# w_out and the second half of w_down: some pairs of row tiles by seven block products in place of eight

## The chip, the core and the metric

The kernel runs on one core of one Trainium2 chip. Five engines work side by side, each through its own queue of instructions: TensorE (PE, matmuls; PEld is its loading of the stationary operand), VectorE (DVE), ScalarE (ACT), GpSimd (POOL) and SyncE (SP, which here issues loads). Times are microseconds of one execution on the device. The metric is that time; before the change its median is 1509.69 us over three runs.

## The reference, cut to what matters

One decoder layer, 256 tokens, model width 2048, float32. The mixer's two halves (state space and attention, 2048 features each) are concatenated and projected by `w_out`; the MLP goes up to 8192 and down again:

```
y_mix = concatenate([y_ssm, y_att], axis=-1)        # (256, 4096)
mix   = einsum('bse,ed->bsd', y_mix, w_out)         # (256, 2048)
h     = h + rmsnorm(mix, norm_mix_post)
hdn   = relu(einsum('bsd,df->bsf', rmsnorm(h, norm_mlp_pre), w_up))
ff    = einsum('bsf,fd->bsd', hdn * hdn, w_down)    # 8192 -> 2048
h     = h + rmsnorm(ff, norm_mlp_post)
```

## The kernel before

Every large product keeps float32 accuracy by splitting both operands into a rounded part (hi, type fp32r) and the rest (lo), and adding three products: hi·hi, hi·lo, lo·hi. `split` (L122) makes the parts: ScalarE writes hi (L125), VectorE subtracts to get lo (L126). Activations are split once and kept: `uh`/`ul` in the tile `u2` (normalised input of a projection), `sh`/`sl` and `ah`/`al` (16 row tiles of 128 features each; `part(k)` finds row tile k of 32).

Weights stream. `fetch` loads two row tiles by 512 columns (512 KB) into one of four `raw` buffers; `weights` (L145) splits them into one of five `hi` and five `lo` buffers. All of that is given a high priority, so the scheduler puts it as far ahead in each queue as buffers let it.

`gemm_tokens` (L170) is the product with tokens in rows: for a block of 512 columns it takes two PSUM banks (one for each tile of 128 tokens) and goes through the row tiles in pairs (KB = 2): per pair 2 token tiles x 2 row tiles x 3 parts = 24 matmuls of 128x512 from two column blocks' view, 12 per column block. `w_out` and each half of `w_down` have 32 row tiles (16 pairs) and four column blocks. Where `lag` is given, the second token tile runs some pairs behind the first, so that the first one's end can be worked on early.

PSUM has eight banks: six in `pacc` (`bank`), two in `psm` (`psmall`). While `w_out`'s first column block runs, attention's last four heads are still going on: each head is a generator in `waiting`, and `pump` runs one step of one head after each pair of row tiles. Then attention's memory is given back and the pool `hp` opens on it: `h` (the residual stream, 2 MB), `mw` (the collected result), `wpost` (the norm's weights, 1 MB broadcast), and `r`, two tiles of 128x512. Their loads are issued by ScalarE (L679, L680).

For each finished column block of `w_out`, `mixed` (L636) sums the squares from PSUM on ScalarE and multiplies by `wpost` on VectorE. After the last one `residual` (L643) scales, adds to `h`, transposes it on TensorE and splits it into `u2` for `w_up`. The second half of `w_down` adds its column blocks to what the first half left in `mw`; `finish` (L716) does the last block and writes the output.

## Time and profile before

| | us |
|---|---|
| median of three runs | 1509.69 (1509.39 to 1510.25) |
| the profiled execution, its own time | 1508.91 |
| its span, first instruction to last | 1507.1 |
| matmuls recorded | 7725 |

The span is what the profile covers; the execution's own time is 1.8 us longer. In the rows of the profile, the first number of a timeline row is its start in us from the span's start, the second its duration in us; x4 means four instructions merged, the duration then runs from the first's start to the last's end. In a row of groups, the numbers behind the bar are busy us in total and mean ns of one. In a row of windows, each engine has its busy us and, in brackets, how many instructions; then come the granted clock of TensorE (1.00 is full), the DMA engines' busy share and GB/s. Where a window was asked for TensorE alone, its column is the only one. In a row of loads the last number is the median time from issue to landing.

### The profile page before, as it was taken

The page shows a single profiled execution, that of the slowest core. Times are in us where ns is not written, and L with a number is a line of the kernel's source. Part 1 is how long each engine was busy: PE and PEld are TensorE (multiplying, and loading weights), DVE is VectorE, ACT ScalarE, POOL GpSimd, SP SyncE. Part 2 cuts the span into 40 slices and gives each one's busy share as a digit, 9 for nine tenths or more (in the row PEclk, how much of TensorE's full clock was granted, in tenths as well). Part 3 has the DMA queues.
Part 4 walks back from the last instruction along what each step waited for, and adds up shares of the span by engine and source line. Part 5 has one row for each costly group of instructions (what it writes and reads, how often), then busy time and mean ns, then how long its engine had stood idle before and what let it go on. Part 6 is the DMA issues. An engine that isn't in the chain of part 4 may idle for free.

```text
span 1507.1 us, 20168 instructions
## 1 busy us (share of the span) xinstructions
PE 1493.2 (99%) x7725; PEld 1275.4 (85%) x7725; DVE 917.5 (61%) x1314; ACT 763.1 (51%) x1063; POOL 56.1 (4%) x73
## 2 busy tenths in 40 slices
PE   9999999999999999999999999999999999999997
PEld 8888888888888888888878888888888888888886
DVE  6988797886555565544457656644444665655444
ACT  7564665554545454544456555543444555544432
POOL 0002200220000000000000000000000000000000
PEclk9999999999999999999999999999999999999999
DMA  7665566556555655475556666555556666655553
GB/s 274 193 205 177 184 183 190 181 155 181 173 177 169 179 169 179 168 266 194 185 167 216 185 189 194 182 195 195 192 189 197 191 185 192 189 189 194 191 174 126
DMA packets 147841, 283.13 MB, mean 188 GB/s; under 512 B 11312, under 2 KB 14240, under 8 KB 147232
## 3 DMA queue, kind: packets, MB, share of 16 engines
q1 hardware_dynamic: 143312, 272.37, 57.4%
q10 hardware_dynamic: 4432, 9.48, 1.8%
q8 instruction: 60, 0.98, 0.3%
q14 instruction: 37, 0.30, 0.1%
HBM read 279.68 MB, written 2.13 MB: 187 GB/s over the span
## 4 chain that ended last, share of the span: by engine, by line
PE 96%; DVE 2%; DMA 1%; ACT 1%; issue 1%; SPq 0%; POOL 0%; POOLq 0%; DVEq 0%; ACTq 0%
PE acc L201 29%; PE acc L187 16%; PE acc L188 16%; PE acc L189 16%; PE acc L204 15%; PE ps L521 1%; DMA raw<-in_w_in_dram 1%; DVE lo L126 1%; PE ps L564 0%; PE ps L586 0%; ACT hi L125 0%; DMA raw_dt<-in_w_in_dram 0%; PE ps L477 0%; PE ps L563 0%; PE ps L587 0%
## 5 line engine op out<-in xcount | busy, mean ns | idle before, releaser
L126 DVE TENSOR_TENSOR lo<-raw,hi 128x1024 fp32r<-128x1024 f32 (+1 forms) x514 | 631.3, 1229 | 527.9 <-ACT hi L125 526.6
L125 ACT ACTIVATE hi<-raw 128x1024 fp32r<-128x1024 f32 (+1 forms) x514 | 542.5, 1056 | 637.7 <-PE acc L189 336.0
L201 PE MATMUL acc<-u,hi 128*128 128x512 f32 x1984 | 539.3, 398 | 1.3 <-DVE u L128 1.2
L201 PEld LDWEIGHTS acc<-u,hi 128*128 128x128 f32 x1984 | 344.8, 189 | 51.4 <-DVE u L128 1.4
L204 PEld LDWEIGHTS acc<-u,lo 128*128 128x128 f32 x1984 | 296.2, 189 | 36.9
L204 PE MATMUL acc<-u,lo 128*128 128x256 f32 x1984 | 305.4, 281 | 0.0
L187 PE MATMUL acc<-hi,sh 128*128 128x512 f32 x384 | 150.5, 392 | 0.0
L187 PE MATMUL acc<-hi,ah 128*128 128x512 f32 x384 | 149.9, 390 | 0.0
L188 PE MATMUL acc<-lo,sh 128*128 128x512 f32 x384 | 149.5, 389 | 0.0
L189 PE MATMUL acc<-hi,sl 128*128 128x512 f32 x384 | 149.4, 389 | 0.0
L189 PE MATMUL acc<-hi,al 128*128 128x512 f32 x384 | 149.4, 389 | 0.0
L188 PE MATMUL acc<-lo,ah 128*128 128x512 f32 x384 | 149.4, 389 | 0.0
L187 PE MATMUL acc<-hi,u 128*128 128x512 f32 x288 | 112.9, 393 | 0.3 <-ACT u L127 0.3
L189 PE MATMUL acc<-hi,u 128*128 128x512 f32 x288 | 112.1, 390 | 0.7 <-DVE u L128 0.7
L188 PE MATMUL acc<-lo,u 128*128 128x512 f32 x288 | 112.1, 390 | 0.0
L188 PEld LDWEIGHTS acc<-lo,sh 128*128 128x128 f32 x384 | 72.1, 188 | 15.0 <-DVE lo L126 0.2
L189 PEld LDWEIGHTS acc<-hi,sl 128*128 128x128 f32 x384 | 72.1, 188 | 15.0
L189 PEld LDWEIGHTS acc<-hi,al 128*128 128x128 f32 x384 | 72.1, 188 | 14.9
L188 PEld LDWEIGHTS acc<-lo,ah 128*128 128x128 f32 x384 | 72.1, 188 | 14.8
L187 PEld LDWEIGHTS acc<-hi,sh 128*128 128x128 f32 x384 | 72.1, 188 | 14.8
L187 PEld LDWEIGHTS acc<-hi,ah 128*128 128x128 f32 x384 | 72.1, 188 | 14.8
L189 PEld LDWEIGHTS acc<-hi,u 128*128 128x128 f32 x288 | 54.1, 188 | 12.4 <-DVE u L128 1.1
(190 smaller groups left out, 940.1 us busy)
## 6 DMA issues: line engine op xcount, KB each, us to landing
raw<-in_w_in_dram SPq DMA_DIRECT2D x190, 512.0 KB, 3.6
raw<-in_w_up_dram SPq DMA_DIRECT2D x128, 512.0 KB, 3.7
raw<-in_w_down_dram SPq DMA_DIRECT2D x128, 512.0 KB, 3.5
raw<-in_w_out_dram SPq DMA_DIRECT2D x64, 512.0 KB, 4.2
bc<-acs_d ACTq DMA_DIRECT2D x8, 512.0 KB, 4.3
xs<-in_x_dram SPq DMA_DIRECT2D x8, 256.0 KB, 6.6
h<-in_x_dram ACTq DMA_DIRECT2D x1, 2048.0 KB, 11.2
raw<-in_w_in_dram SPq DMA_DIRECT2D x4, 256.0 KB, 4.5
```

What stands on the lines that cost most here:

```text
L125: return (nc.scalar.activation(hi, src, AF.Copy), nc.vector.tensor_tensor(lo, src, hi.bitcast(F32), op=ALU.subtract))
L126: nc.vector.tensor_tensor(lo, src, hi.bitcast(F32), op=ALU.subtract))
L187: nc.tensor.matmul(acc[t], a_h[:, r, ts], hi[:, j], start=k == 0, stop=False)
L188: nc.tensor.matmul(acc[t], a_h[:, r, ts], lo[:, j], start=False, stop=False)
L189: nc.tensor.matmul(acc[t], a_l[:, r, ts], hi[:, j], start=False, stop=k == nk - 1)
L201: nc.tensor.matmul(acc[f], hi[:, j, f * P:(f + 1) * P], u2[:, k0 + j], start=k0 + j == 0, stop=False, skip_group_check=True)
L204: nc.tensor.matmul(acc[f][:, 0], lo[:, j, f * P:(f + 1) * P], uh[:, k0 + j], start=False, stop=k0 + j == NK - 1, skip_group_check=True)
L521: nc.tensor.matmul(p[:, c, r], bc[:, r, c * P:(c + 1) * P], xdt[:, c, r], start=True, stop=True)
```

## The change

Two column blocks are now computed together, as one unit: four accumulators `acc` (two token tiles by two column blocks) and four more banks, `more`, so that all eight banks are used. Some pairs of row tiles are then treated as a 2 x 2 by 2 x 2 block product (two token tiles, two row tiles, two column blocks) in the Winograd form of Strassen's scheme: seven block products in place of eight, each of three matmuls. Such a pair (`seven`) needs

- four sums of activation blocks (`sums_of_acts`, L214 to L217 of the changed kernel, then a split). They are written into `u2`, which is not in use then, and kept for the second unit.
- four sums of weight blocks: L234 and L235 (E0 and E1), L236 (B, in place in the second raw tile), L242 (T, in place in the first raw tile), and splits of A, E0 and E1, B, and T. A and B are 128x1024, the others 128x512.

Products that are wanted in several outputs go to `more`; after a unit's last seven `combine_new` (L729 to L733) or `combine_onto` (L740 to L748) brings these into `mw`. So `mixed` now first adds the accumulator to `mw`, and squares and multiplies after that.

In `w_out` the first unit runs pairs 0 to 5 plainly (attention's twelve steps are pumped in these), then pairs 6, 8, 10, 12 by seven and 7, 9, 11 plainly, then 13 to 15 one column block after the other. The second unit has six sevens (2, 4, 6, 8, 10, 12). The second half of `w_down` has four (2, 5, 8, 11) and six (2, 5, 8, 11, 9, 12 in an order of its own): twenty in all.

```diff
+    def sums_of_acts(k, tmp):
+        if k in sums_of:
+            return sums_of[k]
...
+        with tc.high_priority(offset=AHEAD):
+            a, c = (tmp().rearrange("p (i s) -> p i s", s=P) for _ in range(2))
+            ah_, al_ = (v[:, r:r + KB].bitcast(F32).rearrange("p j (t s) -> p (j t) s", t=NT) for v in (h_, l_))
+            nc.vector.tensor_tensor(a, ah_, al_, op=ALU.add)
+            nc.vector.tensor_tensor(c[:, 0:2], a[:, 0::3], a[:, 1:2].to_broadcast([P, 2, P]), op=ALU.subtract)
+            nc.vector.tensor_tensor(c[:, 2], a[:, 0], c[:, 1], op=ALU.add)
+            nc.vector.tensor_tensor(c[:, 3], a[:, 2], c[:, 2], op=ALU.subtract)
+            ch, cl = (u2[:, q + j].rearrange("p b (t s) -> p (b t) s", t=NT) for j in range(KB))
+            split(ch, cl, c)
...
+    def seven(src, ca, cb, k, acc, more, first, last, tmp):
+        ch, cl = sums_of_acts(k, tmp)
+        h_, l_, r = part(k * KB)
+        with tc.high_priority(offset=AHEAD):
+            raw_a = fetch(src, k * KB, ca)
+            raw_b = fetch(src, k * KB, cb)
+            hl_a = parts()
+            split(*hl_a, raw_a)
+            e = [tmp(), tmp()]
+            nc.vector.tensor_tensor(e[0], raw_a[:, 0], raw_b[:, 0], op=ALU.add)
+            nc.vector.tensor_tensor(e[1], e[0], raw_b[:, 1], op=ALU.add)
+            nc.vector.tensor_tensor(raw_b[:, 0], raw_b[:, 0], raw_b[:, 1], op=ALU.add)
+            hl_e = parts()
+            for j in range(KB):
+                split(*(v[:, j] for v in hl_e), e[j])
+            hl_b = parts()
+            split(*hl_b, raw_b)
+            nc.vector.tensor_tensor(raw_a[:, 1], e[1], raw_a[:, 1], op=ALU.add)
+            hl_t = parts()
+            split(*(v[:, 0] for v in hl_t), raw_a[:, 1])
...
+        for dst, (a_h, a_l), (hi, lo), j, own in (
+                (more[0], block(0, 0), hl_a, 0, True), (acc[0], block(1, 0), hl_a, 1, False),
+                (more[1], summed(1), hl_e, 0, True), (more[2], summed(2), hl_e, 1, True),
+                (more[3], summed(0), hl_b, 0, True), (acc[1], summed(3), hl_b, 1, False),
+                (acc[2], block(1, 1), hl_t, 0, False)):
+            nc.tensor.matmul(dst, a_h, hi[:, j], start=own and first, stop=False)
+            nc.tensor.matmul(dst, a_h, lo[:, j], start=False, stop=False)
+            nc.tensor.matmul(dst, a_l, hi[:, j], start=False, stop=own and last)
+
+    def unit(src, n, order, last, acc, more, tmp, combine, lag=0, at_end=(None, None), pumps=1, first=True):
+        cols = (n * NB, (n + 1) * NB)
+        sevens = [k for k, by_seven in order if by_seven]
+        for i, (k, by_seven) in enumerate(order):
+            if by_seven:
+                seven(src, *cols, k, acc, more, k == sevens[0], k == sevens[-1], tmp)
+            else:
+                for b in range(2):
+                    row_tiles(src, cols[b], [k], acc[b::2], part, first and i == 0, False, pumps=pumps)
+            if k == sevens[-1]:
+                combine(more)
+        for b in range(2):
+            row_tiles(src, cols[b], last, acc[b::2], part, False, True, lag if b else 0, at_end[b], pumps)
...
+    def combine_new(n, more):
+        with tc.high_priority(offset=AHEAD):
+            a, b = columns(n), columns(n + 1)
+            u = tmp()
+            nc.scalar.activation(mw[:, 0, a], more[0], AF.Copy)
+            nc.vector.tensor_tensor(u, mw[:, 0, a], more[2], op=ALU.subtract)
+            nc.vector.tensor_tensor(mw[:, 1, a], more[3], u, op=ALU.add)
+            nc.vector.tensor_tensor(mw[:, 0, b], more[1], u, op=ALU.add)
+            nc.vector.tensor_tensor(mw[:, 1, b], more[3], mw[:, 0, b], op=ALU.add)
...
     def mixed(n, t, acc):
-        cs = slice(n * NB, (n + 1) * NB)
+        cs = columns(n)
         with tc.high_priority(offset=2 * AHEAD):
+            nc.vector.tensor_tensor(mw[:, t, cs], acc, mw[:, t, cs], op=ALU.subtract if n % 2 else ALU.add)
             junk = hp.tile([P, NB], BF16, name="junk", bufs=2)
-            nc.scalar.activation(junk, acc, AF.Square, accum_out=ssq[:, t, n:n + 1])
-            nc.vector.tensor_mul(mw[:, t, cs], acc, wpost[:, cs])
+            nc.scalar.activation(junk, mw[:, t, cs], AF.Square, accum_out=ssq[:, t, n:n + 1])
+            nc.vector.tensor_mul(mw[:, t, cs], mw[:, t, cs], wpost[:, cs])
...
-    acc = gemm_tokens(w_out, 0, part, 2 * NK)
+    acc = [bank() for _ in range(2 * NT)]
+    early = 6
+    for k in range(early):
+        for b in range(2):
+            row_tiles(w_out, b * NB, [k], acc[b::2], part, k == 0, False)
...
+    more = [psmall(), bank(), psmall(), bank()]
...
+    unit(w_out, 0, [(k, k in (6, 8, 10, 12)) for k in range(early, 13)], (13, 14, 15), acc, more, tmp,
+         lambda x: combine_new(0, x), 0, (whole(0), whole(1)), first=False)
+    acc, more = more, acc
...
+    unit(w_out, 2, [(k, k in (2, 4, 6, 8, 10, 12)) for k in range(13)], (13, 14, 15), acc, more, tmp,
+         lambda x: combine_new(2, x), LAG_OUT, (third, done), 2)
...
+    unit(w_down[4096:], 0, [(k, k in (2, 5, 8, 11)) for k in range(13)], (13, 14, 15), acc, more, tmp,
+         lambda x: combine_onto(0, x), 0, (complete(0), complete(1)))
+    unit(w_down[4096:], 2, [(k, k in (2, 5, 8, 11, 9, 12)) for k in (0, 1, 2, 3, 5, 4, 8, 6, 11, 7, 9, 10, 12)],
+         (13, 14, 15), more, acc, tmp,
+         lambda x: combine_onto(2, x), LAG_DOWN, (complete(2), finish))
```

`row_tiles` is the old loop of `gemm_tokens` with a list of pairs; its three matmuls stand at L186 to L188 of the changed kernel, those of a seven at L257 to L259. The old kernel's L586 and L587 (a head's last product) are L668 and L669.

Three places show how instructions moved. The first is TensorE at the end of attention, in w_out: the last head's product (`ps<-pT,tk`) and what stands around it. Before:

```order
L187 MATMUL acc<-hi,ah 128x512
L188 MATMUL acc<-lo,ah 128x512
L189 MATMUL acc<-hi,al 128x512
L586 MATMUL ps<-pT,tk 128x256
L587 MATMUL ps<-pT,tk 128x128
L187 MATMUL acc<-hi,ah 128x512
L188 MATMUL acc<-lo,ah 128x512
```

And TensorE at that place in the changed kernel (`u_76` is the tile u2 with the sums of activations):

```order
L186 MATMUL acc<-hi,sh 128x512
L187 MATMUL acc<-lo,sh 128x512
L188 MATMUL acc<-hi,sl 128x512
L668 MATMUL ps<-pT,tk 128x256
L669 MATMUL ps<-pT,tk 128x128
L257 MATMUL ps<-hi,sh 128x512
L258 MATMUL ps<-lo,sh 128x512
L259 MATMUL ps<-hi,sl 128x512
L257 MATMUL acc<-hi,sh 128x512
L258 MATMUL acc<-lo,sh 128x512
L259 MATMUL acc<-hi,sl 128x512
L257 MATMUL acc<-hi,u_76 128x512
```

The first seven (pair 6) follows the last head's product directly, and its third block product reads the sums. VectorE's queue at the same place, where the splits of attention's outputs (`al<-ps`) end. Before:

```order
L126 TENSOR_TENSOR lo<-raw,hi 128x1024
L126 TENSOR_TENSOR al<-ps,ah 128x256
L126 TENSOR_TENSOR lo<-raw,hi 128x1024
L126 TENSOR_TENSOR al<-ps,ah 128x256
L126 TENSOR_TENSOR lo<-raw,hi 128x1024
L641 TENSOR_TENSOR mw<-acc,wpost 128x512 x2
```

VectorE in the changed kernel, from the last heads' splits on (`r` are the small tiles of the pool `hp`):

```order
L126 TENSOR_TENSOR al<-ps,ah 128x256 x3
L214 TENSOR_TENSOR r<-sh,sl 128x512
L126 TENSOR_TENSOR al<-ps,ah 128x256
L215 TENSOR_TENSOR r<-r 128x256
L216 TENSOR_TENSOR r<-r 128x128
L217 TENSOR_TENSOR r<-r 128x128
L234 TENSOR_TENSOR r<-raw 128x512
L236 TENSOR_TENSOR raw<-raw 128x512
L126 TENSOR_TENSOR u_76<-r,u_76 128x512
L126 TENSOR_TENSOR lo<-r,hi 128x512
L235 TENSOR_TENSOR r<-r,raw 128x512
L126 TENSOR_TENSOR lo<-raw,hi 128x1024
```

The first sum stands ahead of the last head's split, everything else of the seven behind it; B's split is the last row shown, and L242, the next pair's L214, E1 and T follow. The third place is VectorE in a cycle of w_out's second unit, one plain pair and one seven with known sums, where before there were only plain splits:

```order
L126 TENSOR_TENSOR lo<-raw,hi 128x1024 x3
L234 TENSOR_TENSOR r<-raw 128x512
L235 TENSOR_TENSOR r<-r,raw 128x512
L236 TENSOR_TENSOR raw<-raw 128x512
L126 TENSOR_TENSOR lo<-r,hi 128x512 x2
L126 TENSOR_TENSOR lo<-raw,hi 128x1024
L242 TENSOR_TENSOR raw<-r,raw 128x512
L126 TENSOR_TENSOR lo<-raw,hi 128x512
```

The first row holds the plain pair's two splits and A's; then come E0, E1, B and, as the last row, T. T's split is the last reader of one of the two raw tiles, so that tile's next load is issued behind it.

## The prediction

> **What bounds the kernel now.** I read the page's first and fourth part, then two windows, for the engine that is never idle and for the room beside it.

> ```profile
> span 1507.1 us, 20168 instructions
> PE 1493.2 (99%) x7725; PEld 1275.4 (85%) x7725; DVE 917.5 (61%) x1314; ACT 763.1 (51%) x1063; POOL 56.1 (4%) x73
> PE 96%; DVE 2%; DMA 1%; ACT 1%; issue 1%; SPq 0%; POOL 0%; POOLq 0%; DVEq 0%; ACTq 0%
> ...
> 1340.00:1440.00 100.00, 100.00 (x443) 1.00 0.57 193
> ...
> 606.00:785.00 179.00, 178.50 (x801) 147.67 (x800) 87.84 (x108) 77.69 (x102) 0.55 (x1) 1.00 0.60 201
> ```

> TensorE is the chain (96%). The fourth row is TensorE alone in w_down: 443 matmuls in 100 us at clock 1.00, one per **0.226 us**. The records' 0.39 us overlap, so a matmul taken out is worth 0.226, not 0.39. The last row is w_out: VectorE works 88 of 179 us. That room is what the change draws on, so VectorE needs its pace too:

> ```profile
> 655.71 4.63 DVE L126 TENSOR_TENSOR lo<-raw,hi 128x1024 fp32r<-128x1024 f32 x4 [0.26 <-ACT hi L125]
> ...
> 1326.06 0.68 DVE L126 TENSOR_TENSOR al<-r,ah 128x512 fp32r<-128x512 f32 x1
> 1326.66 0.68 DVE L737 SCALAR_TENSOR_TENSOR r<-r,rbc 128x512 f32<-128x512 f32 x1
> ...
> 330.31 0.69 DVE L524 TENSOR_TENSOR yg<-ps,xs 128x512 f32<-128x512 f32 x1 [2.16 <-PE ps L521]
> 331.03 0.69 DVE L526 TENSOR_TENSOR yg<-yg,tk 128x512 f32<-128x512 f32 x1
> ...
> 339.67 0.42 DVE L225 TENSOR_TENSOR cT<-acc,cT 128x256 f32<-128x256 f32 x1
> 340.00 0.69 DVE L596 TENSOR_TENSOR cT<-cT,rbq 128x512 f32<-128x512 f32 x1
> ...
> L504 DVE TENSOR_SCALAR bc<-bc,acs 128x128 f32<-128x128 f32 x64 | 13.9, 280 | 0.0
> L125 ACT ACTIVATE ah<-r 128x512 fp32r<-128x512 f32 x16 | 10.1, 633 | 0.5
> ```

> Start to start, a 128x1024 operation takes (4.63-1.23)/3 = 1.13 us, a 128x512 one 0.60, or 0.72 if it reads the one before (330.31 to 331.03), a 128x256 one 0.33. For 128x128 I take 0.28. ScalarE's half of a 128x512 split is 0.63.

> **The gain.** Twenty pairs of row tiles go by seven products: ten in w_out, ten in the second w_down. Each drops 3 of 24 matmuls: 60 x 0.226 = **-13.6 us**. A seven takes TensorE 21 x 0.226 = 4.75 us, a plain pair 5.42, one of each 10.17.

> **The price, on VectorE.** A seven splits A and B (1.13 each), E0, E1 and T (0.60 each) and makes four sums of weights (0.60 each): 6.5 us. New sums of activations add 0.60 + 0.33 + 0.28 + 0.28 + 0.60 = 2.1. The plain pair beside it takes 2.3. One of each is 8.7 us with known sums, 10.9 with new ones, against TensorE's 10.17. In three stretches sevens and plain pairs alternate; only in the first unit of the second w_down are there two plain pairs to a seven (15.6 us for 13.2), and I cost that unit at nothing. ScalarE, about 6.5 us of a cycle, is covered.

> **First unit of w_out, the largest cost.** In VectorE's order (shown with the change) the first sum stands among attention's last splits; its tile lies where attention's tiles were, so it waits for the last head's product. These rows are that moment before, and the loads of it:

> ```profile
> 642.65 0.38 PE L587 MATMUL ps<-pT,tk 128*128 128x128 f32 x2
> 643.38 0.36 ACT L125 ACTIVATE ah<-ps 128x256 fp32r<-128x256 f32 x1
> 644.66 0.42 DVE L126 TENSOR_TENSOR al<-ps,ah 128x256 fp32r<-128x256 f32 x1
> ...
> raw<-in_w_out_dram SPq DMA_DIRECT2D x6, 512.0 KB, 6.6
> h<-in_x_dram ACTq DMA_DIRECT2D x1, 2048.0 KB, 11.2
> wpost<-in_norm_mix_post_dram ACTq DMA_DIRECT2D x1, 1024.0 KB, 7.4
> ...
> raw<-in_w_out_dram SPq DMA_DIRECT2D x39, 512.0 KB, 4.3
> ...
> raw<-in_w_down_dram SPq DMA_DIRECT2D x128, 512.0 KB, 3.5
> ```

> Before, plain products followed that head (its own al came at 644.66 because a weight split was in hand; now the buffers are full by then and VectorE is free). Now the first seven stands right behind it on TensorE, and nothing but A can be prepared ahead. Count from that product's end. VectorE's rows up to T's lo: sum 0.60, al 0.33, the three chained sums 0.45 + 0.31 + 0.31, L234 0.72, L236, lo of the sums, lo of E0, L235 at 0.60 each, B 1.13, L242, the next pair's L214, E1 at 0.60 each: 8.1 us. T's lo ends at 8.7, its last two matmuls at about 9.4, where TensorE alone needs 4.75. **+4.6**.

> The next seven (k=8) needs its second raw tile, whose buffer comes free when T's lo ends. h and wpost (3 MB) load just then; the row for the loads beside them says 6.6 us to landing (4.3 later in w_out). So L234 starts at 8.7 + 0.1 + 6.6 = 15.4, and L234 to T's lo is 0.72 + 4 x 0.60 + 1.13 + 3 x 0.60 + 0.45 = 6.5 us. The seven ends at about 23.2, where TensorE alone has 14.9: another **+3.7**. From T to T it is then 0.69 + 0.1 + 4.3 + 6.5 = 11.6 us by way of the load (11.1 by VectorE's rows alone) against 10.17: two more cycles, less a little since the last has no sums behind it, **+2.4**. After the last seven the first plain split stands behind L730 and L731, which wait for its products: **+1.0**. Sum **+11.7**; its ends are 7.7 (rival 1's price, with the last wait hidden) and 13.1 (landings of 5.0 in the later cycles).

> **The other alternating stretches.** With known sums, T to T is 0.69 + 0.1 + 4.3 for the load, then L234 0.72, four at 0.60, B 1.13 and 1.40 for L242 with ScalarE's half of T: 10.75, 0.6 over TensorE. But there is slack: w_out's second unit has T's lo about 10.4 us behind the first unit's end and needs it at 14.5, so 4.1 us. It goes as 1.4 for one cycle with new sums and 4 x 0.6: 3.8, just covered. The second w_down starts such a stretch with 5.5, and spends 3 x 0.6 and 2 x 1.4, 4.6. I take **+0.5** for both; the ends are 0 and, with landings of 5.6, 10.

> **w_out into w_up.** `mixed` now adds from PSUM first, and the square waits for it:

> ```profile
> 781.82 0.60 ACT L640 ACTIVATE junk<-acc 128x512 bf16<-128x512 f32 x1 [0.30 <-PE acc L189]
> 784.11 0.39 PE L189 MATMUL acc<-hi,al 128*128 128x512 f32 x1
> 784.16 2.08 DVE L651 SCALAR_TENSOR_TENSOR h<-mw,rmix,h 128x512 f32<-128x512 f32 x3 [0.66 <-POOL rmix L634]
> 785.01 0.63 PE L656 MATMUL ps<-cst,h 128*128 128x128 f32 x4 [0.51 <-PE acc L189]
> ```

> Before, the square starts at 781.82 and L651 at 784.16, as TensorE's last matmul does. Now 0.7 comes ahead of the square, and the first L766 (the old L651) also stands behind the second row tile's addition, which ends about 785.2. TensorE waits some **+1.0** longer (0.5 to 1.8). The final tail keeps its operations and waits; the combinations (24 VectorE operations) stand between splits with five buffers of cover: 0 beyond the 1.0 above.

> **Sum.** -13.6 + 11.7 + 0.5 + 1.0 = **-0.4 us**. The profiled execution took 1508.9 us (1507.1 of span); that gives 1508.5. The median of the runs is 0.8 above it, hence **1509.3**.

> **Rivals.** (1) *Landings stay short and VectorE's own pace is the limit.* The second seven then starts L234 at 13.0 and ends at 20.8, and the first unit costs 4.6 + 1.3 + 1.8 + 1.0 = 8.7 with nothing in the other stretches: -13.6 + 8.7 + 1.0 = -3.9, **1505.8**. For it: w_down's 128 loads have a median of 3.5; against it: h and wpost in the rows above. [...]

> (2) *Loads in bursts land later, and the raw buffers bound both alternating stretches.* A cycle issues four loads of 512 KB within about 5 us, then none; before they left 2.7 us apart. From about 4.5 us to landing on, the slack is gone and each 0.1 us costs about 1 us (ten cycles); from about 4.75 the kernel is slower than before by 3 us. At 5.0, 0.7 above the row, w_out's second unit drifts 3.8 + 3.5 against 4.1 of slack (3.2 lost), w_down's 4.6 + 3.5 against 5.5 (2.6), and the first unit's two late cycles lose 1.4: 7.2 in place of 0.5, **1516.0**. For it: 6.6 in the crowded rows. Against it: the mean rate rises only by 24/22.5 (10.17 us for what took 10.84).

> (3) *TensorE's clock falls in the new gaps.*

> ```profile
> 1497.00:1507.00 10.00, 0.89 (x4) 0.39 (x3) 5.36 (x10) 0.72 (x2) 0.92 (x1) 0.78 0.54 197
> ```

> After the last matmul the granted clock is 0.78 over ten us: if it fell to half, that is 4.4 us of it, so it fell some 4.7 us after TensorE went idle. The forecast's longest gap is 2.1 us (A's end at 1.4, E0's hi at 3.5). A gap of over twice that at k=8 would cost about 2 us more: 1511.5. [...]

> **How the numbers follow.** Forecast 0.46, rival 1 0.26, rival 2 0.24, rival 3 0.04. A measurement of this kernel tells about 0.2%, 3 us, from no change: faster (below 1506.7) has rival 1 and the forecast's lower edge, less rival 1's upper part: 0.26; slower (above 1512.7) rival 2 and part of rival 3: 0.28; the same 0.46. The range, 1504.0 to 1516.0, reaches below rival 1 to the first unit's lower end and the transition's (-13.6 + 7.7 + 0.5 = -5.4, 1504.3), and up to rival 2 at landings of 5.0; later landings, under 0.15, stay out.

> **What would show it.** TensorE's records fall by 60 and its pitch stays 0.226. Behind attention's last product TensorE should idle some 4 to 5 us in all within the first seven, released by VectorE's lo or ScalarE's hi, and again 3 to 4 in the second; later sevens of w_out's second unit should run without gaps. w_out, from its first product to its last, should grow by about 5 us (-6.8 + 11.7 + some drift), and the second w_down shrink by about 6.5. The forecast is wrong if w_down's stretch shows gaps at T (rival 2), if the first two sevens cost under 5 us together (rival 1), or if a window of w_out shows a clock under 1.00 (rival 3).

## The result, and the profile after

The changed kernel takes 1524.04 us (median of four runs, 1522.87 to 1530.55) beside 1509.97 us for the kernel before on the same chip (four runs, 1509.39 to 1511.76): a ratio of 1.010, 95% interval 1.007 to 1.013. It is slower by some 14 us, outside the predicted range. The profiled execution took 1522.87 us.

The first and the fourth part of its page:

```profile
span 1521.1 us, 20414 instructions
PE 1491.2 (98%) x7665; PEld 1265.6 (83%) x7665; DVE 1044.7 (69%) x1546; ACT 805.1 (53%) x1139; POOL 57.7 (4%) x73
...
PE 80%; DVE 10%; DMA 5%; ACT 3%; issue 2%; POOL 0%; ACTq 0%; POOLq 0%; DVEq 0%; SPq 0%
```

The 60 matmuls are gone, and yet TensorE's share of the chain fell from 96% to 80%: the other engines and the loads now hold it up. To see where, I cut both executions at the same places of the program: attention's last product, the first product of w_out's second unit, w_out's last product, the first product of the second w_down, that of its second unit, the last product, and the end. The windows between these, for TensorE alone (length, busy time and records, granted clock, DMA share, GB/s); first the kernel before:

```profile
642.65:697.30 54.65, 54.65 (x243) 1.00 0.72 248
697.30:784.11 86.81, 86.81 (x384) 1.00 0.58 189
784.11:1323.52 539.41, 537.75 (x2831) 1.00 0.61 190
1323.52:1410.59 87.07, 87.07 (x387) 1.00 0.57 193
1410.59:1497.50 86.91, 86.91 (x385) 1.00 0.45 155
```

and the changed kernel:

```profile
641.76:704.69 62.93, 56.61 (x231) 0.97 0.68 226
704.69:791.55 86.86, 84.70 (x366) 1.00 0.62 198
791.55:1336.15 544.60, 538.93 (x2830) 1.00 0.62 189
1336.15:1423.70 87.55, 85.30 (x374) 1.00 0.58 188
1423.70:1510.64 86.94, 84.90 (x367) 1.00 0.47 156
1510.64:1521.10 10.46, 0.39 (x2) 0.74 0.54 201
```

A stage should have become shorter by its sevens at 3 x 0.226 us each; what it is longer than that is its loss:

| stage | before | after | sevens' gain | loss | predicted |
|---|---|---|---|---|---|
| up to attention's end | 642.65 | 641.76 | | -0.9 | 0 |
| w_out, first unit behind it | 54.65 | 62.93 | -2.7 | 11.0 | 11.7 |
| w_out, second unit | 86.81 | 86.86 | -4.1 | 4.1 | 0.5 for |
| second w_down, second unit | 86.91 | 86.94 | -4.1 | 4.1 | both |
| w_out's end to the second w_down | 539.41 | 544.60 | | 5.2 | 1.0 |
| second w_down, first unit | 87.07 | 87.55 | -2.7 | 3.2 | 0 |
| last product to the end | 9.60 | 10.46 | | 0.9 | 0 |

The losses sum to 27.6 and the gain to 13.6: +14.0, the difference of the spans. The largest term came out nearly as forecast; five smaller ones make the result. (Each row is one profile of each kernel; how far a stage varies from profile to profile is said at the experiments.) Four places show how they look.

**The first seven.** TensorE's timeline in the changed kernel (start, duration; in brackets the idle time before a row and who ended it):

```profile
643.13 0.40 PE L259 MATMUL acc<-hi,sl 128*128 128x512 f32 x1
645.64 0.50 PE L257 MATMUL acc<-hi,u 128*128 128x512 f32 x1 [2.11 <-ACT hi L125]
646.91 0.51 PE L258 MATMUL acc<-lo,u 128*128 128x512 f32 x1 [0.77 <-DVE lo L126]
...
648.65 0.78 PE L258 MATMUL acc<-lo,u 128*128 128x512 f32 x1 [0.54 <-DVE lo L126]
...
650.08 0.63 PE L259 MATMUL acc<-hi,u 128*128 128x512 f32 x1
...
652.62 0.39 PE L186 MATMUL acc<-hi,sh 128*128 128x512 f32 x1
...
660.68 0.50 PE L258 MATMUL acc<-lo,u 128*128 128x512 f32 x1 [0.87 <-DVE lo L126]
```

A is there, then E0's hi comes 2.1 us late, as the prediction had it. The row at 650.08 is new: a matmul of 0.63 us in place of 0.39, in a window with a granted clock of 0.50. TensorE in windows on the raster of the trace's clock record (3.41 us):

```profile
641.87:645.28 3.41, 1.66 (x9) 1.00 0.64 209
645.28:648.69 3.41, 1.75 (x6) 1.00 0.83 250
648.69:652.10 3.41, 3.41 (x8) 0.50 1.01 430
...
792.05:795.46 3.41, 0.11 (x1) 1.00 0.69 183
795.46:798.88 3.42, 3.42 (x15) 0.50 0.36 129
```

From 648.69 on it is halved for one window, and again from 795.46 on, at the transition into w_up.

**The second units.** The chain of waits through one cycle of w_out's second unit (start, duration, what), from one load to the next; its pieces of issue, 0.05 us and less, are left out:

```profile
740.91 4.06 DMA raw<-in_w_out_dram
744.99 0.70 DVE r L234
745.79 0.63 ACT hi L125
746.44 0.62 ACT hi L125
747.18 1.07 ACT hi L125
748.27 1.23 DVE lo L126
749.50 0.61 DVE raw L242
750.21 0.64 ACT hi L125
750.88 0.70 DVE lo L126
751.60 4.68 DMA raw<-in_w_out_dram
```

It is a closed loop: load, E0 (L234), the hi of E0, E1 and B, B's lo, T (L242), T's hi and lo, and then the load that waits for T's raw buffer. Without the load it takes 6.63 us; with 4.06 it is 10.69, with 4.68 it is 11.31, where TensorE needs 10.17.

The slack that these cycles use up is what lies between the end of T's lo and TensorE's first product with T. Here is that place in w_out's first seven of the unit, and below it one cycle of the second w_down's second unit, in which two splits of plain pairs stand between L234 and L235:

```profile
716.56 0.69 DVE L126 TENSOR_TENSOR lo<-raw,hi 128x512 fp32r<-128x512 f32 x1
719.65 0.39 PE L257 MATMUL ps<-hi,sh 128*128 128x512 f32 x1
...
1438.72 0.69 DVE L234 TENSOR_TENSOR r<-raw 128x512 f32<-128x512 f32 x1 [1.57 <-DMA raw<-in_w_down_dram]
1439.33 2.35 DVE L126 TENSOR_TENSOR lo<-raw,hi 128x1024 fp32r<-128x1024 f32 x2
1441.60 0.68 DVE L235 TENSOR_TENSOR r<-r,raw 128x512 f32<-128x512 f32 x1
```

From the end of one T's lo to the next, with the landing of the load between them in brackets, w_out's unit took 12.58 (4.87), 11.05 (4.41), 10.69 (4.06), 11.31 (4.68) and 11.13 us (4.50), that of the second w_down 13.35 (4.47), 12.02 (4.30), 11.12 (4.30), 11.48 (4.10) and 10.74 us (3.64).

**The transition.** TensorE waits for the new h after w_out's last product (791.55) until 795.35, and runs the transposes at half clock:

```profile
795.35 1.05 PE L771 MATMUL ps<-cst,h 128*128 128x128 f32 x4 [3.41 <-DVE h L766]
```

**The end.** The second token tile's last addition (L846) starts 1.25 us behind the last product (1510.64), since the first one's output rows (L852) stand before it; before, it started 0.49 behind (1497.99 after 1497.50).

```profile
1509.77 2.21 DVE L852 SCALAR_TENSOR_TENSOR h<-mw,rff,h 128x256 f32<-128x256 f32 x4 [0.43 <-POOL rff L716]
...
1511.89 0.69 DVE L846 TENSOR_TENSOR mw<-acc,mw 128x512 f32<-128x512 f32 x1
```

### The profile page after: what moved, and what is told of

Its sections match the earlier page's. It is cut to its first block, busy times and chain, and to the rows that moved or that the text cites. A ratio compares the mean times of both kernels' runs of the same rounds, so it can differ in the third digit from the quotient of the medians.

```text
span 1521.1 us, 20414 instructions
## 1 busy us (share of the span) xinstructions
PE 1491.2 (98%) x7665; PEld 1265.6 (83%) x7665; DVE 1044.7 (69%) x1546; ACT 805.1 (53%) x1139; POOL 57.7 (4%) x73
## 4 chain that ended last, share of the span: by engine, by line
PE 80%; DVE 10%; DMA 5%; ACT 3%; issue 2%; POOL 0%; ACTq 0%; POOLq 0%; DVEq 0%; SPq 0%
PE acc L283 29%; PE acc L286 15%; PE acc L188 10%; PE acc L187 10%; PE acc L186 10%; DVE lo L126 5%; DMA raw<-in_w_down_dram 3%; ACT hi L125 2%; DMA raw<-in_w_out_dram 2%; PE ps L603 1%; DVE raw L242 1%; DVE r L234 1%; PE ps L646 0%; PE ps L668 0%; DVE h L766 0%
## 5 line engine op out<-in xcount | busy, mean ns | idle before, releaser
L126 DVE TENSOR_TENSOR lo<-raw,hi 128x1024 fp32r<-128x1024 f32 (+1 forms) x534 | 642.0, 1206 | 399.8 <-ACT hi L125 395.6
L125 ACT ACTIVATE hi<-raw 128x1024 fp32r<-128x1024 f32 (+1 forms) x534 | 550.5, 1039 | 548.9 <-PE acc L283 238.9
L188 PE MATMUL acc<-hi,u 128*128 128x512 f32 x288 | 112.5, 391 | 1.6 <-DVE u L128 1.6
L186 PE MATMUL acc<-hi,u 128*128 128x512 f32 x288 | 113.2, 393 | 0.0
L186 PE MATMUL acc<-hi,sh 128*128 128x512 f32 x276 | 108.9, 395 | 0.0
L187 PE MATMUL acc<-lo,sh 128*128 128x512 f32 x276 | 107.6, 390 | 0.4 <-DVE lo L126 0.4
L188 PE MATMUL acc<-hi,sl 128*128 128x512 f32 x276 | 107.5, 389 | 0.0
L187 PE MATMUL acc<-lo,ah 128*128 128x512 f32 x252 | 98.4, 390 | 1.4 <-DVE lo L126 1.3
L186 PE MATMUL acc<-hi,ah 128*128 128x512 f32 x252 | 97.6, 390 | 1.4 <-ACT hi L125 1.4
L188 PE MATMUL acc<-hi,al 128*128 128x512 f32 x252 | 98.1, 389 | 0.0
L188 PEld LDWEIGHTS acc<-hi,u 128*128 128x128 f32 x288 | 54.2, 188 | 13.6 <-DVE u L128 2.3
L186 PEld LDWEIGHTS acc<-hi,u 128*128 128x128 f32 x288 | 54.3, 188 | 11.3 <-ACT u L127 0.6
L187 PEld LDWEIGHTS acc<-lo,u 128*128 128x128 f32 x288 | 54.3, 188 | 10.6
L188 PEld LDWEIGHTS acc<-hi,sl 128*128 128x128 f32 x276 | 51.8, 188 | 10.9
L186 PEld LDWEIGHTS acc<-hi,sh 128*128 128x128 f32 x276 | 51.8, 188 | 10.4
L187 PEld LDWEIGHTS acc<-lo,ah 128*128 128x128 f32 x252 | 47.3, 188 | 12.4 <-DVE lo L126 2.6
## 6 DMA issues: line engine op xcount, KB each, us to landing
raw<-in_w_in_dram SPq DMA_DIRECT2D x190, 512.0 KB, 3.6
raw<-in_w_up_dram SPq DMA_DIRECT2D x128, 512.0 KB, 3.8
raw<-in_w_down_dram SPq DMA_DIRECT2D x128, 512.0 KB, 3.6
raw<-in_w_out_dram SPq DMA_DIRECT2D x64, 512.0 KB, 4.4
bc<-acs_d ACTq DMA_DIRECT2D x8, 512.0 KB, 4.6
h<-in_x_dram ACTq DMA_DIRECT2D x1, 2048.0 KB, 8.0
```

The costliest lines, as they stand in the source:

```text
L125: return (nc.scalar.activation(hi, src, AF.Copy), nc.vector.tensor_tensor(lo, src, hi.bitcast(F32), op=ALU.subtract))
L126: nc.vector.tensor_tensor(lo, src, hi.bitcast(F32), op=ALU.subtract))
L186: nc.tensor.matmul(acc[t], a_h[:, r, ts], hi[:, j], start=begin, stop=False)
L187: nc.tensor.matmul(acc[t], a_h[:, r, ts], lo[:, j], start=False, stop=False)
L188: nc.tensor.matmul(acc[t], a_l[:, r, ts], hi[:, j], start=False, stop=end)
```

## Experiments

Theories: A, the raw buffers' loop sets the pace where sevens and plain pairs alternate; B, VectorE's own work does; C, the clock; D, the transition's longer chain; E, the first seven stands too close behind attention. Where medians differ by a few us, the stages of the profiles were compared, not the whole times. A stage varies too: in profiles of kernels with four raw buffers whose edit doesn't touch it, the part up to attention's end took 641.76 to 649.48 us, the second w_down's first unit 86.99 to 89.39 and its second 86.75 to 89.36.

### 1. T apart from the raw tile

```diff
-            nc.vector.tensor_tensor(raw_a[:, 1], e[1], raw_a[:, 1], op=ALU.add)
+            nc.vector.tensor_tensor(e[1], e[1], raw_a[:, 1], op=ALU.add)
...
-            split(*(v[:, 0] for v in hl_t), raw_a[:, 1])
+            split(*(v[:, 0] for v in hl_t), e[1])
```

> T is written over E1 in its own tile, no longer into the first raw tile; the same instructions, but that raw buffer comes free when L242 has read it and not after T's split, about 1.4 us earlier in each seven. Theory A (in the alternating stretches a loop through the raw buffer sets the pace: load, sums, splits, T, load): the loop falls from landing + 6.6 us to landing + 5.3 us, under the 10.17 us of TensorE, so the waits in both second units (4.1 us in w_out's, 3.7 in w_down's) fall under 1 us each, and with loads earlier the wait for h at the end of w_out falls as well: 1513 to 1518 us. Theory B (VectorE's own work of 8.7 us a cycle plus its dependent waits sets the pace): nothing changes by more than 2 us, 1522 to 1525.

Measured 1526.31 us (ratio 1.0105, 1.009 to 1.012): no gain. Taken alone this spoke for B. The chain of waits tells otherwise: it had only moved to the other raw tile. From load to load (754.49 to 765.22) it now runs through the load (3.86), A's hi and lo, L234, the hi of E0, E1 and B, and B's lo, 10.73 us. The second units lose as before (87.46 and 87.95 us long), the first unit of w_down less (85.73 for 87.55). Freeing one buffer earlier is not the same as having more of them; so run 6.

### 2. A longer lead for the first token tile

```diff
-LAG_OUT = 1
+LAG_OUT = 2
```

> In w_out's last column block the second token tile runs two pairs behind the first instead of one, so the first one's end comes 2.7 us earlier; nothing else differs. Theory D (the first token tile's addition, square and multiplication are too long for the 2.7 us of lead): the wait of TensorE for h (3.4 us) falls to about 1 us and the clock is not halved behind it, 1519 to 1521 us. Rival (VectorE is behind at this place, since its splits came late, so the addition stands in its queue however early the product ends): the wait for h stays above 2.5 us, 1523 to 1525.

Measured 1526.87 us (1.0109, 1.009 to 1.0128). The wait for h stayed at 3.26 us, and a second one of 1.05 us came for the other token tile. The rival held as far as it went: however early the product ends, the operations behind it come late. The lead grew by six products only, 1.4 us and not 2.7, and the addition began 3.2 us behind the first tile's last product (793.07, 789.83), since the column block before still had its additions, a split and its multiplications in VectorE's queue.

### 3. w_out's first unit by eight products

```diff
+                if not sevens and k % 2 == 0:
+                    sums_of_acts(k, tmp)
...
-    unit(w_out, 0, [(k, k in (6, 8, 10, 12)) for k in range(early, 13)], (13, 14, 15), acc, more, tmp,
+    unit(w_out, 0, [(k, False) for k in range(early, 13)], (13, 14, 15), acc, more, tmp,
```

(`mixed` takes the column blocks 0 and 1 from PSUM, as before the change.)

> w_out's first unit goes by eight products throughout (12 matmuls more, 2.7 us); its sums of activations are still made, for the second unit, which keeps its six sevens. If the first unit's loss is where the trace has it (10.7 us behind attention's last product), the time falls by 10.7 - 2.7 = 8 us, to about 1516. Rival: the stall only moves, since the sums and splits that are late now are late for the second unit as well: 1519 to 1523.

Measured 1515.31 us (1.0034, 1.0024 to 1.0044; ten runs). The unit behind attention takes 54.65 us, to the hundredth what it took before: its whole loss is gone, and the second unit is not later for it (85.13 us, 2.4 lost). The 11 us belong to the sevens of this unit.

### 4. Eight idle matmuls in the first gap

```diff
+            if first and src is w_out and k == 6 and dst is more[1]:
+                for _ in range(8):
+                    nc.tensor.matmul(dst, block(0, 0)[0], hl_a[0][:, 0], start=True, stop=True)
             nc.tensor.matmul(dst, a_h, hi[:, j], start=own and first, stop=False)
```

> Eight matmuls whose result is never read are put into the first gap of w_out's first seven (2.1 us before E0's hi); they take 1.8 us. Theory C (the clock is halved after a stretch of about 3.4 us in which TensorE worked only half of the time): the window that follows shows clock 1.00 and the first seven loses about 4.0 us instead of 5.6, some 1.6 us less in all. Rival (the clock falls because of the wait itself or the load of the other engines): the window still shows 0.5 and the time stays or grows.

Measured 1526.69 us (one run). The windows of the clock at the first seven:

```profile
646.01:649.43 3.42, 2.04 (x7) 1.00 0.83 247
649.43:652.84 3.41, 2.80 (x11) 1.00 1.00 423
```

The clock stayed at full (1.00) behind a window with 2.04 us of records, where the changed kernel's fell to 0.50 behind one with 1.75, as C expected. The first seven took 9.81 us (642.91 to 652.72) where it had taken 10.72 (641.90 to 652.62). But the unit did not get shorter, 63.78 us for 62.93: the second seven waited 1.23 us for a lo in place of 0.87, and the pair ahead of it 0.42 more. In this place the half clock lay beside the wait for the next loads and cost next to nothing by itself. The changed kernel's own rows agree: B's hi of the second seven (659.60) waited until TensorE's product had ended (659.59), but L236, which waits for those loads and which B's hi needs too, had ended only 0.16 us before. This is one run, and its loads of h and of the first raw tile took 0.8 us longer than in the changed kernel.

### 5 and 6. Split buffers 4, raw buffers 4 or 6

```diff
-BUFS = 5
+BUFS = 4
...
-        raw = wp.tile([P, nk, nb], F32, name="raw", bufs=4)
+        raw = wp.tile([P, nk, nb], F32, name="raw", bufs=6)
```

The control (run 5) has the first edit alone.

> Control for the next kernel: hi and lo buffers 4 each in place of 5, raw buffers 4 as in the changed kernel. A seven holds four of them at once, so splits run less far ahead. Theory A (the raw buffers' loop sets the pace of the alternating stretches): little change there, 1524 to 1530 us. Theory F (the split buffers are what holds VectorE back): all waits of the sevens grow, over 1530.

> Hi and lo buffers 4 each, raw buffers 6 in place of 4 (the memory for both is the same as in the changed kernel). Theory A: loads leave two tiles earlier, so the loop through landing and raw buffer is gone: the second units' waits (4.1 us in w_out, 3.7 in w_down) fall under 1.5 us each, the splits behind w_out's last seven stop waiting for loads, and the wait for h (3.4 us) falls under 2; about 1512 to 1517 us, where the control stays above 1522. Theory B (VectorE and ScalarE in their own order set the pace, 10.7 us from T to T whatever the loads do): within 2 us of the control.

Measured 1522.18 us for the control (one run, a little under the range that A gave it) and 1510.76 for 6 raw buffers (1.0005, 0.9996 to 1.0015; ten runs): 11 us less than the control and 13 less than the changed kernel, with the same work for VectorE. The units of w_out and of the second w_down in it:

```profile
642.26:702.93 60.67, 56.88 (x231) 0.94 0.71 240
702.93:786.69 83.76, 83.40 (x366) 1.00 0.61 197
...
1332.57:1417.11 84.54, 84.54 (x375) 1.00 0.59 193
1417.11:1499.84 82.73, 82.73 (x367) 1.00 0.49 159
```

In the second w_down TensorE is busy all the time, and both units are as short as the removed matmuls make them (87.07 - 2.7 = 84.4, 86.91 - 4.1 = 82.8). w_out's second unit lost 1.0 in place of 4.1. The loads were no faster: their median in the second w_down is 4.6 us to landing in both kernels (54 and 56 loads). So A holds and B falls: what was short were buffers to load into. One expectation missed: the wait for h stayed, 3.24 us.

### 7. The last seven of w_out's second unit taken out

```diff
-    unit(w_out, 2, [(k, k in (2, 4, 6, 8, 10, 12)) for k in range(13)], (13, 14, 15), acc, more, tmp,
+    unit(w_out, 2, [(k, k in (2, 4, 6, 8, 10)) for k in range(13)], (13, 14, 15), acc, more, tmp,
```

> w_out's second unit without its last seven (pair 12 by eight products: 3 matmuls, 0.7 us more), so five plain pairs stand behind its last seven instead of three. Theory D2 (at the end of w_out VectorE is still catching up, so the first token tile's addition waits in its queue): the wait for h falls from 3.4 to about 1 us, the clock is not halved, the last stall of a seven (0.7) goes too: w_out plus transition 4 to 5 us shorter, some 1519 to 1520. Theory D1 (the added operations themselves, addition before square before multiplication, are the cost): the wait for h stays about 3 us, 1523 to 1524.

Measured 1526.43 us (1.0104, 1.0089 to 1.012). The wait for h is 3.24 us again, and w_out with the transition is 0.7 us shorter, not 4 to 5: D2 falls, VectorE is not catching up there. The time is above what D1 gave it because of the second w_down (178.15 us for 174.49), which this edit doesn't touch. Of the theories named, the added operations and their neighbours in the queues are left; run 9 tests them.

### 8. Sums of activations elsewhere in ScalarE's order

```diff
+            if src is not w_out and n == 0 and k == 7:
+                for later in (8, 11):
+                    sums_of_acts(later, tmp)
```

> In the second w_down's first unit the sums of activations for pair 11 are asked for one pair earlier, which puts their hi behind two plain splits and ahead of E0 of the seven at pair 8 in ScalarE's order, instead of ahead of the four plain splits behind that seven. Theory G (ScalarE stood 2.6 us before that hi with the four splits behind it): the waits of TensorE behind the third seven (1.1 for hi, 0.8 for lo, 2.4 us in all) go, and the second unit keeps its own: 1521 to 1522. Rival (the four splits would have waited for their loads anyway): the waits stay above 1.5 us.

Measured 1527.1 us (1.0112, 1.0095 to 1.0129). The two waits behind the third seven went, two smaller ones (0.46 and 0.53) came, and what the first unit gained (86.19 us for 87.55) the second gave back (88.97 for 86.94); both are no larger than these units vary by themselves. With 6 raw buffers that hi stands ahead of the same four splits and nothing is lost, so theory G falls as a cause: the order decided only where the lack of buffers showed.

### 9. The addition at w_out's end on TensorE

```diff
+            if b and add:
+                for t in range(NT):
+                    nc.tensor.matmul(acc[b::2][t], ident, mw[:, t, cols[b]:cols[b] + NB], start=False, stop=False)
...
+            if minus:
+                nc.vector.scalar_tensor_tensor(mw[:, 0, b], more[1], -1.0, u, op0=ALU.mult, op1=ALU.subtract)
+                nc.vector.tensor_tensor(mw[:, 1, b], mw[:, 0, b], more[3], op=ALU.subtract)
+                return
```

In runs 9 and 10 the last column block of w_out's result has the opposite sign, by a factor of -1 in an operation that is there anyway.

> On top of the kernel with 6 raw buffers: for w_out's last column block the collected part is added into the accumulators by TensorE (the combination leaves its negative, two matmuls with the identity put it there before the last three pairs), so that at its end the square and the multiplication read PSUM again, as before the change. Theory D1 (the addition, and the weight split that each engine now runs between addition, square and multiplication, is what delays h): TensorE's wait for h falls from 3.2 us to about 0.5, the clock is not halved there, and the stage from w_out's last product to the second w_down falls from 545.9 to about 540.5; the two matmuls add 0.5 to 2 us to w_out; 1506 to 1509 us. Rival (the lateness comes from elsewhere, from the loads of w_up or the splits): the wait stays above 2 us.

Measured 1508.85 us (0.9992, 0.9982 to 1.0002; ten runs). The end of w_out with the addition on VectorE, in the timeline of run 6 (last product of the first token tile at 783.97, of the second at 786.69):

```profile
785.32 0.68 DVE L753 TENSOR_TENSOR mw<-acc,mw 128x512 f32<-128x512 f32 x1
...
785.81 1.06 ACT L125 ACTIVATE hi<-raw 128x1024 fp32r<-128x1024 f32 x1 [1.66 <-PE acc L188]
786.77 0.61 ACT L755 ACTIVATE junk<-mw 128x512 bf16<-128x512 f32 x1
786.90 1.23 DVE L126 TENSOR_TENSOR lo<-raw,hi 128x1024 fp32r<-128x1024 f32 x1 [0.89 <-ACT hi L125]
...
788.04 0.69 DVE L756 TENSOR_TENSOR mw<-mw,wpost 128x512 f32<-128x512 f32 x1
```

and with it on TensorE, run 9 (last product at 789.16):

```profile
789.25 2.08 DVE L779 SCALAR_TENSOR_TENSOR h<-mw,rmix,h 128x512 f32<-128x512 f32 x3 [0.66 <-POOL rmix L719]
790.06 0.66 PE L784 MATMUL ps<-cst,h 128*128 128x128 f32 x4 [0.52 <-DVE h L779]
```

Above, a weight split stands on each engine in the middle of the chain: its hi ahead of the square, its lo ahead of the multiplication, and that hi had itself waited for TensorE. So 0.6 us of addition became 2.8 us: h started 5.5 us behind the first tile's last product (789.51), before the change 2.8 (784.16 after 781.39, twelve products ahead of the last). Below, TensorE waits 0.52 us (0.51 before the change), the clock stays full (1.00 from 785.20 to 805.68), and the stage is 540.58 us for 545.88. w_out's second unit grew by 2.8 us (86.58 for 83.76); 1.9 of it are the records of the two matmuls with the identity. D1 holds.

### 10. The same, with w_out's first unit plain

The edits of runs 6, 9 and 3 together.

> The same, and w_out's first unit by eight products throughout (its sums of activations are still made for the second unit): sixteen sevens. If the terms add up: w_out falls from 144.4 by the first unit's loss of about 8.5 and grows by 2.7 and by the two matmuls, to 139 to 140; w_up's stage 540.5, the second w_down 167.3, the tail 0.9 over before: 1501 to 1504 us. Rival (the first unit's late start moves into the second, which now has no unit of sevens ahead of it): w_out over 141.5, 1505 or more.

Measured 1502.15 us (0.9948, 0.9934 to 0.9963). The stages added up: w_out 140.15 us, w_up's stage 540.60, the second w_down 167.25.

### 11. The first seven two pairs later

```diff
+                if not first and k == 9:
+                    sums_of_acts(6, tmp)
...
-    unit(w_out, 0, [(k, k in (6, 8, 10, 12)) for k in range(early, 13)], (13, 14, 15), acc, more, tmp,
+    unit(w_out, 0, [(k, k in (8, 10, 12)) for k in range(early, 13)], (13, 14, 15), acc, more, tmp,
```

> 6 raw buffers, nothing else of the two edits above; in w_out's first unit pair 6 goes by eight products (3 matmuls, 0.7 us more), so the first seven is pair 8, two plain pairs (10.8 us) behind attention's last product; its sums of activations for pair 6 are made later, at pair 9. Theory E (the first seven loses because attention's memory holds back everything but A): of the 8.5 us lost in the first unit at least 5 go, w_out 138 to 140, 1505 to 1507 us. Rival H (the loads of h and of the norm's weights and VectorE's rate in this stretch hold it, wherever the first seven stands): the loss only moves to pair 8, w_out over 142.5, 1509 or more.

The edits of run 6 are under it. Measured 1506.57 us (0.9978, 0.9969 to 0.9988; ten runs). w_out takes 139.89 us for 144.43, and of the first unit's loss 3.9 us are left (56.54 us, where 54.65 less three sevens' 2.0 were possible) in place of 8.7: 4.8 us hung on the place behind attention, with the loads of h and the norm's weights unmoved. That is E, a little under the 5 us that it asked for; what the removed seven would have lost anywhere else was not measured apart.

### 12. A version that beats both

Run 10 with the sign that the result needs (4 split buffers, 6 raw buffers, first unit plain, the last addition on TensorE, sixteen sevens).

> The version put together from the runs: hi and lo buffers 4 and raw buffers 6; w_out's first unit by eight products, its sums of activations made for the second; in w_out's last column block the collected part added by TensorE (here with the sign that the result needs); sixteen sevens, of which six in w_out's second unit and ten in the second w_down. By the stages of the runs so far: w_out 140, w_up's stage 540.6, the second w_down 167.3, tail 10.4: 1501 to 1503 us, ratio to the kernel before 0.994 to 0.997. If the rounds put it at 1506 or more, the stages did not add.

Measured **1501.62 us** (five runs, 1501.13 to 1503.09) beside 1510.09 for the kernel before: ratio **0.9944, 95% interval 0.993 to 0.9957**.

## Why the prediction was wrong, point by point

- **The gain, -13.6: right.** 60 records fewer, pitch 0.226. With 6 raw buffers the second w_down got all of its share (167.27 us for 173.98, -6.7).
- **First unit of w_out, +11.7: right in sum and cause (11.0).** The first seven lost 6.0 (10.72 us for 4.76; predicted 4.6), the cycle behind it 2.6 (652.62 to 665.42, 12.80 us for 10.17; predicted 3.7), the rest 2.4 (predicted 2.4 + 1.0). Counted from the end of attention's last product (642.14), T's lo ended at 8.9 us, L234 of the next seven began at 15.3 and that seven ended at 23.3, where the prediction had 8.7, 15.4 and 23.2. Run 3 shows that the loss belongs to this unit's sevens, run 11 that 4.8 of 8.7 us (with 6 raw buffers) hang on the place behind attention. What was missing in the first seven is the half clock, which was hardly on the path (run 4).
- **"The other alternating stretches", +0.5 for both: the step that failed, 8.2 measured.** The loop was drawn rightly (10.75 at a landing of 4.3; the chain shows 10.69 at 4.06). Wrong was "just covered": the slack was set too large and the drift too small. In w_out's second unit the first T's lo ended 2.4 us ahead of its product (717.25, 719.65), not 4.1, and five cycles took 5.9 us more than TensorE's 10.17 each, not 3.8. In the second w_down's second unit it was 4.6 us ahead (1434.10, 1438.66), not 5.5, and the five cycles took 7.9 more, not 4.6. These ends make 6.8 of the 8.2 us; the waits came one split later, and the rest is not worked out. Later landings are only part of it: in w_out's loop the loads took 4.5 us on average for the forecast's 4.3, in w_down's 4.2, no longer than forecast. There the first three cycles spent 8.9, 7.7 and 6.8 us from the landing to the end of T's lo, where the sum has 6.45: in the first two, splits of plain pairs stood between L234 and L235 (2.3 and 1.1 us). So rival 2 was right about the buffers, as run 6 shows (with two more of them the waits went, at the same 4.6 us), and only in part about the landings: the medians of all loads rose (behind attention 5.0 us in w_out, 4.6 in the second w_down), but they count loads on which no cycle waits.
- **"I cost that unit at nothing" (first unit of the second w_down): failed, 3.2 measured.** Two plain pairs give VectorE room, as written, but the unit loads through the same four buffers; with six the loss is 0.2. I had tested it against VectorE's rate alone.
- **"TensorE waits some +1.0 longer (0.5 to 1.8)" into w_up: failed, 5.2 measured.** The term counted the addition and the second tile's addition, but not the weight splits that stand among them: in VectorE's queue a lo of 1.23 us at 790.19 ahead of the first tile's addition (791.33) and one of 1.22 at 791.93 ahead of its multiplication (793.07), and in run 6 also ScalarE's hi of 1.06 us at 785.81 ahead of the square (786.77). The half clock behind the wait (0.50 from 795.46 to 798.88; the first four transposes took 1.05 us for 0.63 before the change) adds to it; how much of the 5.2 is the clock's was not measured apart.
- **"The final tail keeps its operations and waits": 0.9 measured.** The operations are kept; the first token tile's lead is not. The last pairs are now a block of three with a lag of three, so 18 products (4.1 us) follow the first tile's end, where before 24 did (5.4). That is read from the order and the rows above; it wasn't tried.
- **Rival 3** had the clock fall after one long gap and was priced with that. It fell behind a window that held the last 0.4 us of the 2.1 us gap and gaps of 0.8 and 0.5 us (1.75 us of records in 3.41).

Of what would show it, "if w_down's stretch shows gaps at T" and "if a window of w_out shows a clock under 1.00" both came; the gaps showed one split later, at the plain pair behind T. w_out grew by 8.3 us and not by about 5, and the second w_down grew by 0.5 where it should have shrunk by about 6.5.

## What to carry to other kernels

When a change makes loads leave in bursts, test it against the loop from a buffer's release through the load back to that release, not only against each engine's work: here all that a load took longer came back in its cycle (10.69 us at 4.06, 11.31 at 4.68), and so did the splits that stood between its steps; two more buffers were worth 11 to 13 us. An operation added to a chain at a stage's end costs its own time plus whatever the scheduler puts between it and its neighbours in their queues (here 0.6 us became 2.8). And freeing one buffer earlier may only move such a loop to the next buffer.

## What was not expected of the hardware

```profile
1384.74:1388.15 3.41, 1.74 (x7) 1.00 0.52 180
1388.15:1391.56 3.41, 3.41 (x10) 0.50 0.83 269
```
